# A two-layer encoder trunk on one core: the attention's products with v of all four blocks of rows in one group behind both softmaxes, with five buffers for transposed probabilities

## The chip, the cores and the metric

The kernel runs on one core of a Trainium2 chip. The core has a matrix engine (TensorE, PE in the profile; its loads of weights are PEld), a vector engine (DVE), a scalar engine (ACT), a general engine (GpSimd, POOL) and an engine that here only starts DMAs (SP). Each takes its own instructions in a fixed order and waits for the others by semaphores. The metric is the time of one execution on the device, in microseconds (us). The kernel before took 1608.74 us, the median of three runs (1607.14 to 1610.86).

## What is computed

Two groups of 512 tokens (group 0, group 1) go through the same two layers of width 1024: a bidirectional recurrent layer, then a gated neighbourhood attention with 16 heads of 64. The part that matters here, from the reference:

```python
qr = lax.dynamic_index_in_dim(qg, r, axis=1, keepdims=False)
kr = lax.dynamic_slice_in_dim(kb, rs, win_r, axis=1)
vr = lax.dynamic_slice_in_dim(vb, rs, win_r, axis=1)
...
s = jnp.einsum('bnqhd,bsnkhd->bhnqsk', qr, kr, preferred_element_type=f32)
s = jnp.where(mask, s + bias.astype(f32), NEG_INF)
p = jax.nn.softmax(s.reshape(s.shape[:4] + (-1,)), axis=-1).reshape(s.shape)
return jnp.einsum('bhnqsk,bsnkhd->bnqhd', p.astype(v.dtype), vr)
...
return (o.reshape(bsz, t, D_INNER) * jax.nn.silu(z)) @ w_o + b_o
```

The tokens stand in a grid of 8 rows and 64 columns, and every token attends to a window of 8 rows and 16 columns around it.

## The kernel before

**Layout.** The kernel keeps activations as 128 channels by 512 tokens, the tokens ordered by grid column. 128 channels are two heads, a *pair*; there are eight pairs in each group. A pair's 512 queries are four *blocks* of 128 tokens (16 grid columns), n = 0 to 3, and each block attends to 256 tokens that begin at column 0, 8, 24 or 32 (`cols`).

**One pair** is the generator `heads(s, p)`, s the group, p the pair:

- It loads the bias and q, k, v of the pair (DMAs from SP), transposes v (L1573) and copies it to `vtok` (L1574). `vtok` has seven slots of 128 tokens; the copy fills the even ones, and two DMAs from POOL (L1575, L1576) put together the odd ones, which hold tokens shifted by 64. Block n reads the slots `cols[n] // 8` and that plus 2: 0 and 2, 1 and 3, 3 and 5, 4 and 6.
- For each half, blocks (0, 1) and then (2, 3): four products q by k, two heads for each of two blocks, into a bank `sc` (L1588). Then for each block and head the softmax: bias and maximum (L1599), exponential and sum on ACT (L1602), reciprocal (L1603) and scaling (L1604) on DVE, and two transposes of 128 by 128 into a bank `pt` (L1606). ACT copies the transposed probabilities of a block, both heads, to a buffer `pts` (L1609).
- Then the eight products with v of the half (L1621) into the pair's one bank `po`, the block with the higher number first (`ns[::-1]`). Each product appears in the profile as two records, since its operands are 32-bit floats: a half is 16 records.
- Behind the second half, `po` is multiplied with the gate z (L1630), and the result is split into two halves of reduced precision (`os`) for the product with the attention's output matrix (`out1` for group 0, `last` for group 1).

The long products that all other matrix products consist of are three for each 128 channels of input (L457 to L459, in `last` L1708 to L1710): 128 by 128 weights by 512 columns. The products of a pair with 64 rows or 64 columns use a part of the array each, so the two heads run side by side: in the profile 64*128 for the scores and 128*64 for the products with v.

**Buffers.** The banks of this phase are `pg` 2, `pt` 2 (`PG, PT`), `po` 1, `sc` 1, `pm` 1. `pts` has three buffers (`NPT`), `vtok` two (`NK`), the softmax rows `sb` four (`NSB`). A buffer is written again when all who read it are done.

**What sets the order.** In this phase the order on each engine isn't written out by hand. A planner works it out when the kernel is built: it goes through simulated time and puts in line on each engine, among the instructions whose inputs and buffers are ready, the one with the best priority, which is the place in the source unless it is raised. `high_priority(HPA)`, 1000 places, raises the scores and the products with v; `behind(one, last)` keeps the order inside such a group. Transposes and copies have their place in the source.

**How it is interleaved.** In `rest`, generators of long products are advanced, and between their steps the attention's generator is advanced by some share: `run(g, (a, 0.9))` advances `a` 0.9 steps for each step of `g`. A step of `g` is three long products. For group 0, six pairs are queued at first; the input products of pairs 6 and 7 (32 steps each at 0.9, so 28 attention steps each) and group 1's first-layer output product (`out0(1)`, 64 steps at 1.0) carry 120 attention steps. A pair takes 15 steps. Behind `out0(1)`, what is left of the queue is emptied (`while queue: next(a)`), and then come `out1(0)` and group 1's norm. For group 1, the input products of one pair carry the attention of the pair before, 21 steps (32 at 0.66) for a pair in the middle, and the rest is emptied before `last`.

Of the kernel before, what the change touches and what calls it, by code (L numbers as in the profile page):

```python
# [20 lines left out]
P = 128  # L21
# [233 lines left out]
class Trunk:  # L255
# [8 lines left out]
    POST4 = 0.2  # L264
    TOK = True
    LAST = ("pg", "pg", "po", "pm")
    PG, PT, NK, NPT = 2, 2, 2, 3
    AHEAD, AHEADW, SCAN_A, SCAN_W = 0, 0, 300, 300
    NAB, NX, NR, NY, NSB, NBI = 2, 2, 2, 2, 4, 2
    NAK, NZ = 1, 1  # L270
# [1289 lines left out]
    def heads(self, s, p):  # L1560

        nc = self.nc
        vt, act, gps = nc.vector, nc.scalar, nc.gpsimd
        a = lambda tag, shape=(P, T), n=1, dt=F32: self.t(tag, shape, n, dt, self.ap)
        bias = a("bias", (P, 2, 3, 256), self.NBI)
        for h in range(2):
            self.load(bias[:, h].rearrange("p a b -> p (a b)"), self.a["rpb"][2 * p + h])
        q, k, v = (self.load(a(kind, n=2), self.sp[kind, s, p]) for kind in ("q1", "k1", "v1"))
        yield
        vtok = a("vtok", (P, 7, P), self.NK)  # L1570
        ps = self.p("pm", (P, 4, P))
        for j in range(4):
            nc.tensor.transpose(ps[:, j], v[:, j * P:(j + 1) * P], self.ident)  # L1573
        act.copy(vtok[:, 0:7:2], ps)  # L1574
        nc.gpsimd.dma_start(vtok[0:64, 1:6:2], vtok[64:128, 0:5:2])  # L1575
        nc.gpsimd.dma_start(vtok[64:128, 1:6:2], vtok[0:64, 2:7:2])  # L1576
        yield
        op = self.p("po", (P, 4, P))
        cols = (0, 8, 24, 32)
        for ns in ((0, 1), (2, 3)):  # L1580

            scs = self.p("sc", (P, 2, 2, 256))
            with self.tc.high_priority(self.HPA):
                last = None
                for n in ns:
                    for h in range(2):
                        hs = slice(64 * h, 64 * h + 64)
                        one = nc.tensor.matmul(  # L1588
                            scs[:, h, n % 2], q[hs, n * P:(n + 1) * P], k[hs, 8 * cols[n]:8 * cols[n] + 256], start=True, stop=True)
                        if last is not None:  # L1590
                            self.behind(one, last)
                        last = one
            pts = []
            for n in ns:
                pt = self.p("pt", (P, 2, 2, P))
                for h in range(2):
                    sb = a("sb", (P, 256), self.NSB)
                    mx = a("mx", (P, 4), 6)
                    vt.tensor_tensor_reduce(  # L1599
                        sb, scs[:, h, n % 2], bias[:, h, (0, 1, 1, 2)[n]], 1.0, -3.0e38, op0=ALU.add, op1=ALU.max, accum_out=mx[:, 0:1])  # L1600
                    vt.tensor_scalar(mx[:, 1:2], mx[:, 0:1], -1.0, None, op0=ALU.mult)  # L1601
                    act.activation(sb, sb, AF.Exp, bias=mx[:, 1:2], accum_out=mx[:, 2:3])  # L1602
                    vt.reciprocal(mx[:, 3:4], mx[:, 2:3])  # L1603
                    vt.tensor_scalar(sb, sb, mx[:, 3:4], None, op0=ALU.mult)  # L1604
                    for e in range(2):
                        nc.tensor.transpose(pt[:, h, e], sb[:, e * P:(e + 1) * P], self.ident)  # L1606
                    yield
                pts.append(a("pts", (P, 2, 2, P), self.NPT))
                act.copy(pts[-1], pt)  # L1609
                if n % 2 == 0:  # L1610
                    yield
            if ns[1] == 3:
                while ("z1", s, p) not in self.sp:
                    yield
                z = self.load(a("z1"), self.sp["z1", s, p])
            with self.tc.high_priority(self.HPA):
                last = None
                for n in ns[::-1]:
                    for e in range(2):
                        for h in range(2):  # L1620
                            one = nc.tensor.matmul(  # L1621
                                op[64 * h:64 * h + 64, n], vtok[:, cols[n] // 8 + 2 * e, 64 * h:64 * h + 64], pts[n % 2][:, h, e],
                                start=(e == 0), stop=(e == 1))
                            if last is not None:
                                self.behind(one, last)
                            last = one
            yield
        with self.tc.high_priority(self.HP[s] if p == NP - 1 else 0):
            o = self.tmp()
            vt.tensor_tensor(o, op.rearrange("p n t -> p (n t)"), z, op=ALU.mult)  # L1630
            lo, hi = (self.t("os", (P, T), 2 * NP, F32R, self.ap) for _ in range(2))
            o = self.halves(o, lo, hi)
        self.os[s].append(o)
        yield
# [447 lines left out]
```

## Time and profile before

| | us |
|---|---|
| median of three runs | 1608.74 |
| the profiled execution | 1607.96 |
| its span | 1606.2 |
| PE busy | 1512.5 |
| DVE busy | 1221.5 |
| ACT busy | 968.3 |
| attention of group 0, with long products, 1115 to 1274 | 159 |
| `out1(0)` and the norm of group 1, 1274 to 1339 | 65 |
| attention of group 1, with long products, 1339 to 1567 | 228 |

The span is the time between the first and the last instruction in the profile; the execution's time has some 2 us around it. Times in rows of the profile are from the span's start. A timeline's row has the start, the duration, the engine, the line of the kernel, the operation, output and inputs by the program's names, the form and the number of instructions merged into the row; a row of several instructions lasts from the first one's start to the last one's end. PE's instructions are pipelined, so the start of the next row tells more than a row's duration.

### The profile page before, as it was taken

What the parts mean: (1) busy time and instruction counts of PE and PEld (TensorE: products, weight loads), DVE (VectorE), ACT (ScalarE), POOL (GpSimd) and SP (SyncE); (2) the same over time, 40 slices, a digit from 0 to 9 for tenths busy, and PEclk for the clock granted to TensorE, in tenths of its full rate; (3) what the DMA queues carried; (4) which work ended last, traced back from release to release, by engine and by line L of the source; (5) the groups of instructions that cost most, each with busy time, mean ns of one, the idle gap of its engine ahead of it and who ended that gap; (6) DMA issues with size and microseconds to landing.
All of it is one profiled execution on the core that took longest, in us unless ns stands there. A gap on an engine that the chain in (4) does not pass through costs nothing.

```text
span 1606.2 us, 46435 instructions
## 1 busy us (share of the span) xinstructions
PE 1512.5 (94%) x18756; PEld 1170.9 (73%) x18756; DVE 1221.5 (76%) x2714; ACT 968.3 (60%) x1931; POOL 199.3 (12%) x368
## 2 busy tenths in 40 slices
PE   7998789998898999998999999999999999999998
PEld 6866667776666777766677777777777788777776
DVE  8996578689889798878799998655767585764664
ACT  6667455856757466676577665544667665554562
POOL 0000114301111012221000011000110002111110
PEclk9999899999999999999999999999999999999999
DMA  6359577777776787768777765465775347665553
GB/s 245 105 187 314 206 251 243 230 238 227 222 257 204 229 260 259 228 209 290 239 252 252 244 223 182 159 199 191 259 226 179 117 151 244 205 195 187 169 169 110
DMA packets 183670, 343.61 MB, mean 214 GB/s; under 512 B 25888, under 2 KB 58912, under 8 KB 183456
## 3 DMA queue, kind: packets, MB, share of 16 engines
q1 hardware_dynamic: 158272, 256.75, 50.1%
q0 software_dynamic: 25184, 83.90, 14.6%
q8 instruction: 147, 2.41, 0.6%
q14 instruction: 67, 0.55, 0.1%
HBM read 230.33 MB, written 107.09 MB: 210 GB/s over the span
## 4 chain that ended last, share of the span: by engine, by line
PE 68%; DVE 11%; DMA 9%; ACT 6%; issue 5%; SPq 0%; POOL 0%; DVEq 0%; ACTq 0%; POOLq 0%
PE pm L937 7%; PE pg L459 7%; PE pg L457 6%; PE pg L458 6%; PE pm L939 5%; PE pm L938 5%; PE pf L1249 3%; PE sc L1588 2%; PE po L1621 2%; PE pt L1606 2%; PE us L1368 2%; DMA cab<-dab 2%; DMA dab<-ab 2%; DVE ab L1071 2%; PE zy L457 2%
## 5 line engine op out<-in xcount | busy, mean ns | idle before, releaser
L937 PE MATMUL pm<-act,whi 128*128 128x512 f32 x672 | 296.0, 440 | 5.3 <-ACT vs L796 2.8
L939 PE MATMUL pm<-act,wlo 128*128 128x512 f32 x672 | 268.7, 400 | 12.8 <-DVE wlo L858 12.8
L938 PE MATMUL pm<-act,whi 128*128 128x512 f32 x672 | 268.3, 399 | 4.0 <-DVE act L884 3.9
L937 PEld LDWEIGHTS pm<-act,whi 128*128 128x128 f32 x672 | 128.6, 191 | 46.7 <-issue 10.8
L939 PEld LDWEIGHTS pm<-act,wlo 128*128 128x128 f32 x672 | 128.8, 192 | 43.7 <-DVE wlo L858 14.9
L457 PE MATMUL pg<-act,whi 128*128 128x512 f32 x384 | 156.5, 408 | 0.0
L459 PE MATMUL pg<-act,wlo 128*128 128x512 f32 x384 | 152.9, 398 | 0.0
L458 PE MATMUL pg<-act,whi 128*128 128x512 f32 x384 | 152.3, 397 | 0.0
L407 DVE TENSOR_TENSOR wlo<-raw,whi 128x512 fp32r<-128x512 f32 x150 | 102.7, 687 | 63.2 <-ACT whi L406 57.9
L938 PEld LDWEIGHTS pm<-act,whi 128*128 128x128 f32 x672 | 129.2, 192 | 28.4 <-DVE act L884 6.3
L406 ACT CAST whi<-raw 128x512 fp32r<-128x512 f32 x150 | 92.4, 617 | 94.5 <-PE pg L458 64.1
L858 DVE TENSOR_TENSOR wlo<-raw,whi 128x512 fp32r<-128x512 f32 x166 | 113.3, 684 | 29.5 <-ACT whi L856 28.3
L856 ACT CAST whi<-raw 128x512 fp32r<-128x512 f32 x166 | 102.2, 619 | 32.9 <-PE pm L938 25.2
L459 PEld LDWEIGHTS pg<-act,wlo 128*128 128x128 f32 x384 | 72.1, 188 | 18.2 <-issue 4.0
L1148 DVE TENSOR_TENSOR N<-etmp,N 128x30 f32<-128x30 f32 (+14 forms) x240 | 78.9, 329 | 4.6
L1146 DVE TENSOR_TENSOR etmp<-N 128x30 f32<-128x30 f32 (+14 forms) x240 | 78.7, 328 | 4.4
L458 PEld LDWEIGHTS pg<-act,whi 128*128 128x128 f32 x384 | 72.4, 189 | 13.1 <-issue 1.0
L457 PEld LDWEIGHTS pg<-act,whi 128*128 128x128 f32 x384 | 72.2, 188 | 12.5 <-issue 0.7
L1602 ACT ACTIVATE sb<-sb,mx 128x256 f32<-128x256 f32 x128 | 64.1, 503 | 19.8 <-DVE mx L1601 19.1
L1249 PE MATMUL pf<-cab 64*64 64x128 f32 (+1 forms) x2048 | 68.3, 269 | 0.8 <-issue 0.4
L1360 ACT COPY X<-us 64x256 f32<-64x256 f32 x128 | 46.8, 365 | 28.8 <-PE zy L1227 24.8
L1031 ACT ACTIVATE th<-pm,dv 128x512 f32<-128x512 f32 x64 | 43.9, 686 | 30.0 <-PE pm L1028 29.5
(402 smaller groups left out, 3501.7 us busy)
## 6 DMA issues: line engine op xcount, KB each, us to landing
dab<-ab POOLq DMA_DIRECT2D x32, 1024.0 KB, 7.4
cab<-dab SPq DMA_DIRECT2D x64, 512.0 KB
raw<-in_w_in_dram SPq DMA_DIRECT2D x128, 256.0 KB
bias<-in_rpb_dram SPq DMA_DIRECT2D x32, 384.0 KB
raw<-in_w_z_dram SPq DMA_DIRECT2D x32, 256.0 KB
raw<-in_w_k_dram SPq DMA_DIRECT2D x32, 256.0 KB
raw<-in_w_r_dram SPq DMA_DIRECT2D x32, 256.0 KB
k<-dk SPq DMA_DIRECT2D x32, 256.0 KB
```

Source lines behind the costliest of these rows:

```text
L406: self.nc.scalar.copy(hi, src)
L407: (eng or self.nc.vector).tensor_tensor(lo, src, hi.bitcast(F32), op=ALU.subtract)
L457: nc.tensor.matmul(ps, hi, x[k][0], start=(k == 0), stop=False)
L458: nc.tensor.matmul(ps, hi, x[k][1], start=False, stop=False)
L459: self.mm = nc.tensor.matmul(ps, lo, x[k][0], start=False, stop=(k == KT - 1))
L856: nc.scalar.copy(hi, raw[h])
L858: nc.vector.tensor_tensor(lo, raw.pop(h), hi.bitcast(F32), op=ALU.subtract)
L937: nc.tensor.matmul(ps, hi[:, at], xh, start=(k == 0), stop=False)
L938: nc.tensor.matmul(ps, hi[:, at], xl, start=False, stop=False)
L939: nc.tensor.matmul(ps, lo[:, at], xh, start=False, stop=(k == KT - 1))
L1148: vt.tensor_tensor(N[:, q + 1:, :q], tv, N[:, q + 1:, :q], op=ALU.add)
L1249: end = nc.tensor.matmul(st.f[half(a), h, 0, d, g] if st.last else st.f[half(a), h, :, d, g], ab[half(h), d, g, 2 * e[d] + 1 - a], rt if s ...
```

## The change

`pts` gets five buffers instead of three. The two groups of eight products with v are taken out of the loop over the halves; behind the loop stands one group of sixteen, which goes through the blocks in rising order, and reads `pts[n]` of the pair's four instead of `pts[n % 2]` of the half's two. The bank `po` is taken where that group begins and not at the pair's start. The wait for z and its load stand in front of the group as before. There is a `yield` behind each half, and one more behind the products, so a pair takes 16 steps.

```diff
-    PG, PT, NK, NPT = 2, 2, 2, 3
+    PG, PT, NK, NPT = 2, 2, 2, 5
...
-        op = self.p("po", (P, 4, P))
-        cols = (0, 8, 24, 32)
+        cols, pts = (0, 8, 24, 32), []
         for ns in ((0, 1), (2, 3)):
...
-            pts = []
             for n in ns:
                 pt = self.p("pt", (P, 2, 2, P))
...
-            if ns[1] == 3:
-                while ("z1", s, p) not in self.sp:
-                    yield
-                z = self.load(a("z1"), self.sp["z1", s, p])
-            with self.tc.high_priority(self.HPA):
-                last = None
-                for n in ns[::-1]:
-                    for e in range(2):
-                        for h in range(2):
-                            one = nc.tensor.matmul(
-                                op[64 * h:64 * h + 64, n], vtok[:, cols[n] // 8 + 2 * e, 64 * h:64 * h + 64], pts[n % 2][:, h, e],
-                                start=(e == 0), stop=(e == 1))
-                            if last is not None:
-                                self.behind(one, last)
-                            last = one
             yield
+        while ("z1", s, p) not in self.sp:
+            yield
+        z = self.load(a("z1"), self.sp["z1", s, p])
+        op = self.p("po", (P, 4, P))
+        with self.tc.high_priority(self.HPA):
+            last = None
+            for n in range(4):
+                for e in range(2):
+                    for h in range(2):
+                        one = nc.tensor.matmul(
+                            op[64 * h:64 * h + 64, n], vtok[:, cols[n] // 8 + 2 * e, 64 * h:64 * h + 64], pts[n][:, h, e],
+                            start=(e == 0), stop=(e == 1))
+                        if last is not None:
+                            self.behind(one, last)
+                        last = one
+        yield
         with self.tc.high_priority(self.HP[s] if p == NP - 1 else 0):
             o = self.tmp()
             vt.tensor_tensor(o, op.rearrange("p n t -> p (n t)"), z, op=ALU.mult)
```

## The prediction

> **What bounds the kernel now.** I read the page's busy shares first, then the busy times by stage, then the chain of work that ended last over the two attention stages, and last the timelines of TensorE (PE) and ScalarE (ACT) inside two pairs.
>
> ```profile
> span 1606.2 us, 46435 instructions
> PE 1512.5 (94%) x18756; PEld 1170.9 (73%) x18756; DVE 1221.5 (76%) x2714; ACT 968.3 (60%) x1931; POOL 199.3 (12%) x368
> 1115.00:1274.00 159.00, 159.00 (x995) 123.80 (x993) 107.92 (x399) 104.39 (x249) 16.10 (x27) 1.00 0.64 212
> 1339.00:1567.00 228.00, 228.00 (x1299) 178.69 (x1298) 142.45 (x457) 125.82 (x287) 32.08 (x56) 1.00 0.60 194
> 1567.00:1599.00 32.00, 31.92 (x137) 25.30 (x136) 15.60 (x29) 7.74 (x19) 0.00 (x0) 1.00 0.33 113
> ```
>
> The last three rows are stages: their length, then the busy time of PE, its weight loads, VectorE, ACT and GpSimd, the granted clock, the DMA share. The first two hold the attention of the two groups. PE is busy in all 159 and all 228 us, at full clock, and stays so until 1599, some 7 us before the end; VectorE and ACT have a third of the time free. The chain agrees:
>
> ```profile
> by line: PE pg L459 19.7%; PE pg L458 19.6%; PE pg L457 19.6%; PE sc L1588 12.4%; PE po L1621 10.3%; PE pt L1606 10.3%; PE pm L1573 2.2%; PE pm L939 2.0%; PE pm L937 1.9%; PE pm L938 1.9%; PE pm L485 0.4%
> ```
>
> That is the first group's stage: every entry is PE. So here time is what PE's instructions take back to back. An engine's wait that PE doesn't share is worth nothing, and whatever makes PE's own sequence longer is paid in full.
>
> **What a bunch of products with v costs PE.** The long products (L457 to L459) and the transposes (L1606) use the array as 128*128, the products with v (L1621) as 128*64, the scores (L1588) as 64*128.
>
> ```profile
> 1475.60 0.40 PE L458 MATMUL pg<-act,whi 128*128 128x512 f32 x1
> 1475.93 1.09 PE L1621 MATMUL po<-pts,vtok 128*64 128x128 f32 x16
> 1476.95 0.50 PE L459 MATMUL pg<-act,wlo 128*128 128x512 f32 x1
> 1477.29 0.39 PE L457 MATMUL pg<-act,whi 128*128 128x512 f32 x1
> 1477.52 0.40 PE L458 MATMUL pg<-act,whi 128*128 128x512 f32 x1
> ...
> 1229.67 0.70 PE L1588 MATMUL sc<-k,q 64*128 64x256 f32 x2
> 1230.30 1.10 PE L1621 MATMUL po<-pts,vtok 128*64 128x128 f32 x16
> 1231.32 1.13 PE L1588 MATMUL sc<-k,q 64*128 64x256 f32 x6
> 1232.38 0.87 PE L1606 MATMUL pt<-cc,sb 128*128 128x128 f32 x6
> ```
>
> Undisturbed, long products start 0.23 us apart (1477.29 to 1477.52). Around the bunch, 1475.60 to 1477.29 is 1.69 us for two of them, so the bunch takes 1.69 - 0.46 = 1.23 us: 1.02 between its own start and the next product's, and 0.21 around it. What of the 1.02 is work? The scores tell: two records (one product of 256 columns in two passes) took 0.63 us, six took 1.06. Six are two rounds, since the two heads run side by side; so a round costs 0.43 and a bunch 0.20 on top. A product with v has half the columns, so a round of 0.215, and sixteen records are four rounds: 0.86 of work, 0.16 of fixed cost. A bunch that stands alone thus costs **0.16 + 0.21 = 0.37 us** beyond its work; one that adjoins scores, only the 0.16.
>
> A rule of the Trainium skill stands behind this row: "TensorEngine Tiling (Array Packing)", section Key Properties, says that a change of the tiling mode, unlike a change of tile, drains the array. Two changes at the skill's constant of about 166 ns for one warm product ("TensorE: Matmul & The Clock Gate", section Single matmul latency) would make an estimate of 0.33 us, and 22 bunches 7.3 us where my rows will say 8.1.
>
> **The change part by part.** The arithmetic is the same: 16 products with v for each pair, as many scores, transposes, copies, DMAs. What moves is (1) the place of the products of the first two blocks, (2) their order, (3) the number of buffers, (4) one step of the generator.
>
> (1) and (2) decide. In the source there is one bunch of 16 products where there were two of 8. But the planner sets PE's order, and what it does with a product at raised priority can be read. Of a pair in the first group:
>
> ```profile
> 1240.58 0.59 ACT L1609 COPY pts<-pt 128x512 f32<-128x512 f32 x1 [0.29 <-PE pt L1606]
> 1244.02 0.58 ACT L1609 COPY pts<-pt 128x512 f32<-128x512 f32 x1
> 1250.75 1.07 ACT L1609 COPY pts<-pt 128x512 f32<-128x512 f32 x2 [1.47 <-PE pt L1606]
> ...
> 1247.35 1.13 PE L1588 MATMUL sc<-k,q 64*128 64x256 f32 x6
> 1248.41 1.09 PE L1621 MATMUL po<-pts,vtok 128*64 128x128 f32 x16
> 1249.43 0.70 PE L1588 MATMUL sc<-k,q 64*128 64x256 f32 x2
> 1255.70 1.09 PE L1621 MATMUL po<-pts,vtok 128*64 128x128 f32 x16
> ```
>
> and of a pair in the second:
>
> ```profile
> 1467.87 0.59 ACT L1609 COPY pts<-pt 128x512 f32<-128x512 f32 x1
> 1471.28 0.57 ACT L1609 COPY pts<-pt 128x512 f32<-128x512 f32 x1
> 1476.00 0.56 ACT L1609 COPY pts<-pt 128x512 f32<-128x512 f32 x1
> 1479.43 0.58 ACT L1609 COPY pts<-pt 128x512 f32<-128x512 f32 x1
> ...
> 1484.48 1.09 PE L1621 MATMUL po<-pts,vtok 128*64 128x128 f32 x16
> ```
>
> The products follow the copy of the probabilities they read by a steady distance: 1244.02 to 1248.41 is 4.4 us, the second copy of the double row (about 1251.3) to 1255.70 also 4.4, 1471.28 to 1475.93 (quoted above) 4.7, 1479.43 to 1484.48 5.1. And three scores of four stand ahead of the bunch at 1248.41 and one behind it: the planner cuts into a group as soon as something is ready. So raised products go where their operand gets ready, not where the source has them. Each half today stands as one bunch of 16 records because its order is backwards: the block whose copy is last goes first. The change counts upwards, block 0 first, and block 0 is ready while three softmaxes are still to come. Nothing else holds it: the output bank is freed by the multiplication with z of the pair before, which follows that pair's last products within 0.2 us of their end (1272.35 and 1273.50, quoted below).
>
> I therefore expect the products of each block about 4.7 us behind their own copy. In the second group's pair that is four bunches of 8 records: 1472.6, 1476.0, 1480.7, 1484.2. In the first group's pair, three: block 0 alone, block 1, and blocks 2 and 3 together, as their copies are back to back and block 3 is ready by the time block 2 has been put in line. Copies that are back to back show as a row with x2:
>
> ```profile
> 1143.08 1.08 ACT L1609 COPY pts<-pt 128x512 f32<-128x512 f32 x2 [2.82 <-PE pt L1606]
> ...
> 1561.03 1.05 ACT L1609 COPY pts<-pt 128x512 f32<-128x512 f32 x2
> ```
>
> These are the first and the last of nine such rows among the 64 copies. One more couple would join: blocks 0 and 1 of the very last pair, whose output bank is held until the pair before is multiplied with z:
>
> ```profile
> 1557.50 0.68 DVE L1630 TENSOR_TENSOR tmp<-po,z 128x512 f32<-128x512 f32 x1
> 1560.11 1.09 PE L1621 MATMUL po<-pts,vtok 128*64 128x128 f32 x16
> ```
>
> That makes 64 - 9 - 1 = **54 bunches where there are 32**, 22 more. At 0.37 us each: **+8.1 us**. The bounds of one more bunch are 0.16 us (it happens to adjoin scores, +3.5 in all) and the scores' own 0.20 + 0.21 = 0.41 (+9.0); I take 0.37, since block 0 and most of the others would stand among long products, like the bunch at 1475.93.
>
> Scores beside the products: today a split into 2 and 6 records costs 0.63 us, as each part pays a round and a drain. Block 1's products meet the scores at the same point as now, so these splits stay; I put nothing. Block 2's products, put in first, could open a new split in front of block 3; at worst 0.63 us in some eight pairs, 5 us; below nothing, one split less here or there, -2.
>
> (3) Five buffers instead of three: the copies don't wait for a buffer today but in the last pair, where the double row at 1561.03 stands behind the products at 1560.11. PE is full there, so a copy that is earlier hides behind long products: nothing. Without that cover it would be worth the copy's 0.58 us.
>
> (4) Each pair now takes 16 steps instead of 15, against 28 + 28 + 64 = 120 steps that the long products of the first group's stage give out: eight pairs needed exactly these 120. Eight steps of the last pair now come behind all of the second group's product with w_o. A step there is three long products, 0.69 us, so its end may slip by up to 5.5 us. Behind it wait the first products of the attention's output matrix:
>
> ```profile
> 1272.35 1.09 PE L1621 MATMUL po<-pts,vtok 128*64 128x128 f32 x16
> 1273.50 0.69 DVE L1630 TENSOR_TENSOR tmp<-po,z 128x512 f32<-128x512 f32 x1 [1.70 <-PE po L1621]
> 1274.87 0.69 DVE L407 TENSOR_TENSOR os<-tmp,os 128x512 fp32r<-128x512 f32 x1 [0.69 <-ACT os L406]
> 1279.20 0.62 PE L457 MATMUL pg<-os,whi 128*128 128x512 f32 x2
> ```
>
> The last pair's slice is complete at 1274.87 + 0.69 = 1275.6, and it is first needed at 1279.20, when both columns that have a bank have used up everything else: 3.6 us of cover. I take nothing, since what gets ready is put in line at once, wherever the source has it; the bounds are 0 and 5.5 - 3.6 = 1.9 us.
>
> **The sum:** +8.1. Of the profiled execution, whose time was 1607.96 us around its span of 1606.2, that makes 1616.1; the median of the three runs, 1608.74, is 0.8 above it, so of the median 1616.8.
>
> **The rivals.**
>
> *One bunch, as the source has it (faster).* If a product can't be put in line before the whole bunch's position is reached, 16 bunches vanish. Seven of today's first bunches adjoin scores (0.16 each), nine don't (0.37): 1.1 + 3.3. With the bunch go the splits of scores into 2 and 6 records around it, four at 0.63 us, of which this is the first and the one at 1247.35 the last; together -7 us, 1601.7.
> ```profile
> 1175.39 0.70 PE L1588 MATMUL sc<-k,q 64*128 64x256 f32 x2
> ```
>
> It decides from the point at which block 0's products are still behind block 3's copy. Against it: the scores of the next half, which the source has behind these products, get ahead of them at 1247.35.
>
> *Block 0 waits for v.* Odd slots of the transposed v come by two DMAs; block 1 needs them, block 0 doesn't. If it is made to wait all the same, blocks 0 and 1 go together in seven pairs of the second group: 15 more bunches, +5.5, 1614.2.
>
> *More splits or a stall between the groups.* The upper ends above: +8.1 + 5 + 1.9, at most 1623.8.
>
> *Hidden in PE.* A busy PE is modelled, and weight loads fill only 178.69 of 228 us (78%); if PE had slack between its products, the extra bunches would fall into it and the time stay at 1608.7. Against it: the starts 0.23 us apart on both sides of the bunch, widened by the whole of it. The Trainium skill, "Perfetto Trace Analysis", section Identifying the Most-Contended Engine, says to judge TensorE's headroom by weight loads, not by matmul time; by that rule a fifth of the stage is free and this rival would win.
>
> **How the numbers follow.** Forecast 0.62, with a range of its own of 1611.5 to 1621; block 0 waiting 0.12; more splits or a stall 0.08; hidden, or so few new bunches that it comes to the same, 0.09; one bunch 0.09. The range leaves out the one bunch and the far end of the splits, and reaches down into the hidden case: 1607 to 1622. A change under 0.2%, 3.2 us, can't be told from none in this kernel. Slower by more: 0.62 + 0.12 + 0.08, less a little for cheap bunches, 0.79; the same 0.12; faster 0.09.
>
> **What would show it.** L1621 in bunches of 8 records and single ones of 16, 54 or so in number and none of 64 records or of 32; block 0's about 4.7 us behind its copy; PE still busy throughout both stages, each longer, the first by some 3 us and the second by 5; an unchanged 7 us behind the last product. The prediction is wrong if the products of a pair stand in one row of 32 records, if the long products beside a short bunch show no gap, or if PE shows idle time around 1280.

## The result and the profile after

The changed kernel took 1625.35 us, the median of four runs (1624.13 to 1626.73); the kernel before, run beside it, took 1607.94, also the median of four runs (1606.85 to 1610.86). The ratio is 1.0112, 95% interval 1.0091 to 1.0133: **17.4 us slower**. The forecast was 8.1 us slower, so the direction came true and the size is over twice as large; it is also more than the 15 us that the prediction's worst rival allowed (8.1 + 5 + 1.9). Behind the change's edits the products with v are on L1620, the transposes on L1604, their copies on L1607, the scores on L1587.

The page of the changed kernel, its span and busy times:

```profile
span 1622.4 us, 46445 instructions
PE 1522.2 (94%) x18756; PEld 1164.7 (72%) x18756; DVE 1223.0 (75%) x2714; ACT 972.8 (60%) x1931; POOL 199.9 (12%) x368
```

The number of PE records is the same as before, and DVE, ACT and POOL are busy for less than 5 us more: no work was added. To see where the time lies, take **the stretch** from the first long product of the attention phase (the first L457 that writes into `pg`) to the start of the last one. It holds all of the attention and all long products beside it. The busy times by window over this stretch (start and end, length, then PE, its weight loads, DVE, ACT, POOL, granted clock, DMA share, GB/s), first of the kernel before:

```profile
1123.77:1598.52 474.75, 474.75 (x2704) 374.88 (x2703) 306.74 (x958) 274.36 (x619) 51.48 (x89) 1.00 0.57 186
```

and of the kernel after:

```profile
1121.51:1614.71 493.20, 490.69 (x2704) 373.33 (x2703) 307.91 (x958) 277.47 (x619) 51.67 (x89) 1.00 0.55 179
```

The stretch grew by 18.45 us. The spans of these two profiles differ by 16.2, since the stretch also began 2.3 us earlier. Nearly all of it is PE: 15.9 us more busy and 2.5 us idle, where there was no idle time at all. The granted clock in the stretch is 1.00 in both. What follows the last product is 7.7 us in both (1606.2 - 1598.52 and 1622.4 - 1614.71).

PE's timeline shows the mechanism that the prediction named. A pair of the second group, first the copies of the probabilities on ACT:

```profile
1478.98 0.59 ACT L1607 COPY pts<-pt 128x512 f32<-128x512 f32 x1 [0.29 <-PE pt L1604]
1482.22 0.59 ACT L1607 COPY pts<-pt 128x512 f32<-128x512 f32 x1 [1.02 <-PE pt L1604]
1487.70 0.59 ACT L1607 COPY pts<-pt 128x512 f32<-128x512 f32 x1 [0.61 <-PE pt L1604]
1491.02 0.58 ACT L1607 COPY pts<-pt 128x512 f32<-128x512 f32 x1
```

then PE's products with v of the same pair, with the long products on both sides of the first:

```profile
1483.17 0.39 PE L459 MATMUL pg<-act,wlo 128*128 128x512 f32 x1
1483.49 0.66 PE L1620 MATMUL po<-pts,vtok 128*64 128x128 f32 x8
1484.08 0.50 PE L457 MATMUL pg<-act,whi 128*128 128x512 f32 x1
1484.42 0.40 PE L458 MATMUL pg<-act,whi 128*128 128x512 f32 x1
...
1486.36 0.66 PE L1620 MATMUL po<-pts,vtok 128*64 128x128 f32 x8
...
1492.20 0.66 PE L1620 MATMUL po<-pts,vtok 128*64 128x128 f32 x8
...
1495.51 0.66 PE L1620 MATMUL po<-pts,vtok 128*64 128x128 f32 x8
```

Four bunches of 8 records, 4.5, 4.1, 4.5 and 4.5 us behind their own copies. The first has a long product 0.32 us ahead of it and the second long product after it starts 0.34 us behind the first: 1483.17 to 1484.42 is 1.25 us, of which two long products take 0.46 and two rounds of products 0.43, so 0.36 us is the price of this bunch.

In a pair of the first group the scores are among them:

```profile
1215.20 0.66 PE L1620 MATMUL po<-pts,vtok 128*64 128x128 f32 x8
1216.84 0.70 PE L1587 MATMUL sc<-k,q 64*128 64x256 f32 x2
1217.46 0.66 PE L1620 MATMUL po<-pts,vtok 128*64 128x128 f32 x8
1218.05 1.13 PE L1587 MATMUL sc<-k,q 64*128 64x256 f32 x6
1221.14 0.66 PE L1620 MATMUL po<-pts,vtok 128*64 128x128 f32 x8
1226.03 0.66 PE L1620 MATMUL po<-pts,vtok 128*64 128x128 f32 x8
...
1228.25 0.38 PE L1604 MATMUL pt<-cc,sb 128*128 128x128 f32 x2
1228.38 0.48 PE L457 MATMUL pg<-act,whi 128*128 128x512 f32 x1
...
1229.17 0.38 PE L1604 MATMUL pt<-cc,sb 128*128 128x128 f32 x2
```

Block 1's products again cut a group of scores (2 and 6 records). And the transposes come two records at a time among long products, where the kernel before had eight in a row:

```profile
1250.06 1.09 PE L1606 MATMUL pt<-cc,sb 128*128 128x128 f32 x8
```

The waits of PE over the stretch, as its timeline shows them in brackets, are these four:

```profile
1288.54 0.51 PE L457 MATMUL pg<-os,whi 128*128 128x512 f32 x1 [0.85 <-ACT oa L1643]
...
1572.83 1.10 PE L1620 MATMUL po<-pts,vtok 128*64 128x128 f32 x16 [1.02 <-DVE tmp L1629]
...
1574.65 0.98 PE L1604 MATMUL pt<-cc,sb 128*128 128x128 f32 x6 [0.37 <-DVE sb L1602]
...
1576.38 0.50 PE L1709 MATMUL pg<-act,os 128*128 128x512 f32 x1 [0.27 <-DVE os L407]
```

**A ledger of the stretch.** Every PE row of the stretch is charged with the time from its start to the next row's start, and each long product's time beyond 0.2285 us, about what it takes undisturbed, goes to the neighbour beside which it stands. In us:

| | before | after | difference |
|---|---|---|---|
| products with v, in 32 bunches, then 61 | 32.79 | 37.18 | +4.4 |
| long products ahead of and behind them, without idle time | 2.70 | 7.49 | +4.8 |
| scores, in 38 groups, then 42 | 37.42 | 40.24 | +2.8 |
| long products around scores | 3.06 | 4.03 | +1.0 |
| all transposes, in 111 groups, then 137, and the long products around them | 40.94 | 42.82 | +1.9 |
| idle | 0 | 2.5 | +2.5 |
| all else (the remainder) | | | +1 |

So there are 29 more bunches, at (4.4 + 4.8) / 29 = 0.32 us each: 9.2 us. The other half is in three places that the prediction put at nothing or didn't cost: the scores, the transposes and the idle time.

### The profile page after: what moved, and what is told of

The parts are those of the page before. It is cut to its first block, busy times and chain, and to the rows that moved or that the text cites. A ratio compares the mean times of both kernels' runs of the same rounds, so it can differ in the third digit from the quotient of the medians.

```text
span 1622.4 us, 46445 instructions
## 1 busy us (share of the span) xinstructions
PE 1522.2 (94%) x18756; PEld 1164.7 (72%) x18756; DVE 1223.0 (75%) x2714; ACT 972.8 (60%) x1931; POOL 199.9 (12%) x368
## 3 DMA queue, kind: packets, MB, share of 16 engines
q0 software_dynamic: 25184, 83.90, 14.5%
## 4 chain that ended last, share of the span: by engine, by line
PE 55%; DVE 8%; DMA 6%; issue 3%; ACT 3%; SPq 0%; POOL 0%; DVEq 0%; ACTq 0%; POOLq 0%
PE pg L457 6%; PE pg L459 6%; PE pg L458 6%; PE pm L937 5%; PE pm L938 4%; PE pm L939 4%; PE sc L1587 2%; PE pf L1249 2%; PE po L1620 2%; PE us L1368 2%; PE pt L1604 2%; PE zy L1321 1%; DMA cab<-dab 1%; PE zy L1372 1%; PE us L1348 1%
## 5 line engine op out<-in xcount | busy, mean ns | idle before, releaser
L457 PE MATMUL pg<-act,whi 128*128 128x512 f32 x384 | 162.1, 422 | 0.0
L458 PE MATMUL pg<-act,whi 128*128 128x512 f32 x384 | 152.8, 398 | 0.0
L407 DVE TENSOR_TENSOR wlo<-raw,whi 128x512 fp32r<-128x512 f32 x150 | 102.7, 687 | 57.8 <-ACT whi L406 43.7
L459 PEld LDWEIGHTS pg<-act,wlo 128*128 128x128 f32 x384 | 72.2, 188 | 17.4 <-issue 2.7
L457 PEld LDWEIGHTS pg<-act,whi 128*128 128x128 f32 x384 | 72.3, 188 | 16.0 <-issue 5.9
L1600 ACT ACTIVATE sb<-sb,mx 128x256 f32<-128x256 f32 x128 | 64.3, 503 | 30.6 <-DVE mx L1599 30.2
L1597 DVE CUSTOM_DVE_ANT_0 sb<-sc,bias 128x256 f32<-128x256 f32 x128 | 50.8, 421 | 29.1 <-PE sc L1587 17.5
```

What stands on the lines that cost most here:

```text
L407: (eng or self.nc.vector).tensor_tensor(lo, src, hi.bitcast(F32), op=ALU.subtract)
L457: nc.tensor.matmul(ps, hi, x[k][0], start=(k == 0), stop=False)
L458: nc.tensor.matmul(ps, hi, x[k][1], start=False, stop=False)
L459: self.mm = nc.tensor.matmul(ps, lo, x[k][0], start=False, stop=(k == KT - 1))
```

## The experiments

Whole times are set against runs of the kernel before that were taken beside them, so its median differs a little from one comparison to the next; the ratios and their intervals come from all the runs and need not be the quotient of the medians. The stretch is always set against the one profile of the kernel before. Whole times vary by several us from run to run, but the stretch hardly does (the last section shows it), so each kernel is judged by both.

**Only the order turned.** The kernel before, its two halves and its three buffers kept, the lower block first:

```diff
-                for n in ns[::-1]:
+                for n in ns:
```

> The kernel before with one edit: inside each half the products with v go through the blocks upwards (0, 1 and 2, 3) instead of backwards. Nothing is moved, three buffers, 15 steps. Theory A (the time is what PE pays for every bunch of products, 0.37 us where it stands alone, and 0.63 us for every split of scores): the order on PE now has 61 bunches instead of 32, by these prices about +13 us, so 1621 (1618 to 1623). Rival B (the cost comes from the place behind both softmaxes, the later bank or the five buffers): no change, 1608. Rival C (the cost comes from the 16th step, which lets the last pair of the first group end late): no change, 1608.

It took 1622.72 us against 1608.26: ratio 1.0096 (1.0064 to 1.0128), +14.5 us.

```profile
1120.42:1608.77 488.35, 487.64 (x2705) 371.46 (x2703) 307.36 (x958) 275.20 (x619) 51.58 (x89) 1.00 0.57 181
```

Of the 18.45 us of the stretch this one word makes 13.6, with 61 bunches as after the change. The lines of a pair of the first group read like the changed kernel's:

```profile
1228.16 0.66 PE L1621 MATMUL po<-pts,vtok 128*64 128x128 f32 x8
1229.81 0.70 PE L1588 MATMUL sc<-k,q 64*128 64x256 f32 x2
1230.43 0.66 PE L1621 MATMUL po<-pts,vtok 128*64 128x128 f32 x8
1231.02 1.13 PE L1588 MATMUL sc<-k,q 64*128 64x256 f32 x6
```

**The place kept, the order turned back.** The changed kernel, each half's later block first:

```diff
-            for n in range(4):
+            for n in (1, 0, 3, 2):
```

> The changed kernel with one edit: the blocks in the order 1, 0, 3, 2, which is the order of before, but all behind both softmaxes, with five buffers and 16 steps. Theory A: each couple's later block goes first, so 32 bunches as in the kernel before and about its time, 1608, plus at most 2.5 us of idle PE at the ends of the groups: 1606 to 1611. Rival B: the place is as in the changed kernel, so 1625. Rival C: 1611 or more, all of it idle time of PE around the first group's end.

1610.91 us against 1608.26: ratio 1.0015 (0.999 to 1.0039). The stretch is 475.77 us, 1.0 longer than before, with 32 bunches again. In this order the place behind both softmaxes, the later bank, five buffers and the 16th step together are worth about 1 us, of which 0.8 is idle. What makes the changed kernel slow needs the rising order.

**The last block first.** The changed kernel, wholly backwards:

```diff
-            for n in range(4):
+            for n in (3, 2, 1, 0):
```

> The changed kernel with one edit: the blocks go downwards, 3 to 0, so the block whose copy is last goes first. Theory A: nothing can be put in line before the last copy, so 16 bunches of 32 records; by the prices -5 us against the kernel before, and up to 2.5 us of idle PE at the ends: 1602 to 1606. Rival B: place, bank and buffers are as in the changed kernel, so 1625. Rival C: some 1611, with the first group's last pair late.

1609.01 us against 1608.26: ratio 1.0007 (0.9981 to 1.0033). That misses the gain expected of it. The bunches did join, 16 of 32 records, and PE is busy for 5.1 us less in the stretch; but 3.2 us of it are idle, so the stretch is only 1.9 us shorter, which the scatter of the whole times hides. In the profiled execution the stretch also began 8 us later than before, ahead of the attention:

```profile
1131.87:1604.71 472.84, 469.67 (x2705) 374.74 (x2703) 307.57 (x958) 275.50 (x619) 51.51 (x89) 1.00 0.58 187
```

Most of the idle time stands at the ends of the two groups, where the norm waits for DVE, and then `out1` of group 0 and `last` of group 1 wait for a bank to come free:

```profile
1285.24 0.91 PE L499 MATMUL pm<-tmp,ones 128*128 128x128 f32 x6 [1.08 <-DVE tmp L495]
1288.62 0.50 PE L457 MATMUL pg<-os,whi 128*128 128x512 f32 x1 [0.84 <-ACT oa L1643]
...
1574.79 0.50 PE L1707 MATMUL po<-h,os 128*128 128x512 f32 x1 [0.79 <-DVE tmp L1629]
```

That points to the 16th step, which the next three take apart.

**Rising order with 15 steps.** The changed kernel, without the step behind the second half:

```diff
-            yield
+            if ns[0] == 0:
+                yield
```

> The changed kernel with one edit: no step behind the second half, so that a pair takes 15 steps as before; blocks upwards, one group behind both softmaxes, five buffers. Theory A: the order on PE has 61 bunches and as many splits of scores as the run with only the halves turned upwards; PE's busy time in the stretch from the first product of the input projection to the end is 488 us as there, and the time 1621 (1618 to 1623): of the change's 18 us some 3 busy and 2 idle belong to the 16th step. Rival B (the place behind both softmaxes, the later bank, the buffers cost by themselves): as the changed kernel, 1625.

1619.52 us against 1605.71: ratio 1.0081 (1.0052 to 1.0111). The stretch is 487.80 us, 5.4 shorter than after the change and 0.5 shorter than with only the order turned, and both have 61 bunches and 40 groups of scores:

```profile
1131.26:1619.06 487.80, 487.41 (x2704) 371.57 (x2703) 307.53 (x958) 275.47 (x619) 51.58 (x89) 1.00 0.55 181
```

So the 16th step costs 5.4 us here: 2.1 of idle time, 2.5 in scores (40.24 - 37.75 in the ledger, two groups more), the rest around them. Place, bank and buffers cost nothing.

**Only the 16th step.** The kernel before, with one more step ahead of the multiplication with z:

```diff
+        yield
         with self.tc.high_priority(self.HP[s] if p == NP - 1 else 0):
```

> The kernel before with one edit: one more step behind the products with v, so 16 for a pair. Theory A: 32 bunches and one split of scores less, so PE is busy for the same 475 us; the last pair of the first group ends later and PE idles 0 to 2.5 us around it: 1607 to 1611. If the 16th step by itself is the larger part of the change's cost: 1616 or more.

1607.81 us against 1605.71: ratio 1.001 (0.9984 to 1.0035). The stretch is 476.74 us, +2.0, of which 1.8 is idle:

```profile
1286.82 0.50 PE L457 MATMUL pg<-os,whi 128*128 128x512 f32 x1 [0.84 <-ACT oa L1645]
...
1566.50 0.63 PE L1606 MATMUL pt<-cc,sb 128*128 128x128 f32 x4 [0.93 <-DVE sb L1604]
```

By itself the step makes the idle time and no new splits. Here it stands behind the products with v, in the changed kernel ahead of them; the run in the order 1, 0, 3, 2, with the step where the changed kernel has it, has no new splits either (37 groups of scores, 38 before). So the splits need the rising order too.

**Only the buffers.** The kernel before with five buffers:

```diff
-    PG, PT, NK, NPT = 2, 2, 2, 3
+    PG, PT, NK, NPT = 2, 2, 2, 5
```

> The kernel before with five buffers for transposed probabilities in place of three, nothing else. Theory A: PE's order is the same instruction for instruction, so 1608, with 474.7 us of PE in the stretch from the first product of the input projection. Rival B (buffers): a difference beyond 3 us to either side.

1607.43 us against 1605.71: ratio 1.0001 (0.9976 to 1.0026). The stretch is 474.69 us against 474.75. In the kernel before, two more buffers do nothing.

**The last block first, with 15 steps.** Both edits, the falling order and 15 steps, on the changed kernel:

```diff
-            yield
+            if ns[0] == 0:
+                yield
...
-            for n in range(4):
+            for n in (3, 2, 1, 0):
```

> The changed kernel with two edits: blocks downwards, 3 to 0, and no step behind the second half, so that a pair takes 15 steps as before. Theory A: 16 bunches of 32 records, fewer splits of scores than in the run with 16 steps (2 instead of 6 or so); by the prices -7.7 us against the kernel before: 1599 to 1602. Rival B: 1625. Rival C: as before, 1608, since with 15 steps nothing is late and a bunch costs nothing.

1600.50 us against 1608.26: ratio 0.9951 (0.9928 to 0.9974), **7.8 us faster than before**. The same kernel, measured a second time:

> The kernel with blocks downwards and 15 steps once more, in more rounds, since its first measurement spread over 17 us. Theory A: PE's stretch from the first product of the input projection to the last product 468.9 us as there, 6 us less than in the kernel before, and the time 4 to 9 us less. If the first result was chance: within 3 us.

gave 1599.68 against 1606.34, ratio 0.9956 (0.9931 to 0.9981). The stretches of the two:

```profile
1124.84:1593.71 468.87, 467.70 (x2704) 374.94 (x2703) 304.85 (x958) 275.15 (x619) 51.55 (x89) 1.00 0.59 188
```

```profile
1124.75:1593.33 468.58, 467.47 (x2705) 375.00 (x2703) 304.80 (x958) 274.97 (x619) 51.54 (x89) 1.00 0.57 189
```

They are 5.9 and 6.2 us shorter than before. A bunch now holds all four blocks, with unsplit scores and eight transposes in a row beside it:

```profile
1237.63 1.97 PE L1621 MATMUL po<-pts,vtok 128*64 128x128 f32 x32
1239.53 1.13 PE L1587 MATMUL sc<-k,q 64*128 64x256 f32 x8
1240.60 1.09 PE L1604 MATMUL pt<-cc,sb 128*128 128x128 f32 x8
```

This version beats both kernels. What the change's source seems to say, one bunch behind both softmaxes, is worth a gain when the block that gets ready last goes first and the pair keeps its 15 steps. Even so 1.1 to 1.2 us of its stretch are idle, most of it a wait for a bank in `out1`, as with 16 steps.

**As many bunches as possible.** The changed kernel with the products with v no longer raised, so that they take their place in the source among the long products:

```diff
-        with self.tc.high_priority(self.HPA):
+        with self.tc.high_priority(0):
```

> The changed kernel with one edit: the products with v get no raised priority, so the planner puts the long products between them: 173 bunches, most of a single product (two records), 141 more than before; the scores aren't split at all (32 groups). Theory A: at 0.37 us a bunch, less 4 us for splits that are gone: +49 us against the kernel before, 1657 (1645 to 1668). Rival (what costs is the splits of scores and idle PE, not the bunches): 1604 to 1612.

1672.99 us, the median of two runs, against 1605.71: ratio 1.0403 (1.0335 to 1.0472). The stretch is 538.36 us, +63.6, with 173 bunches, 143 of them one product of two records:

```profile
1470.35 0.43 PE L1620 MATMUL po<-pts,vtok 128*64 128x128 f32 x2
1470.71 0.49 PE L457 MATMUL pg<-act,whi 128*128 128x512 f32 x1
1471.14 0.43 PE L1620 MATMUL po<-pts,vtok 128*64 128x128 f32 x2
```

The price of a bunch holds far from 32 and 61, but the expected 49 us fell short. A product that stands alone has no product of the other head beside it, so it takes a whole round of 0.215 us where a pair of them shares one: 143 times 0.107 is 15.3 us, and 49 + 15.3 = 64.3, against 63.6 measured. From bunch to bunch is 0.79 us with one long product of 0.23 between: 0.56 us for one product with v. This reason was formed behind the run, but the rows bear it out. From the bunch's start to the next long product is 0.36 us here, 0.59 for a bunch of 8 records (1483.49 to 1484.08, after the change) and 1.02 for one of 16 (1475.93 to 1476.95, before). Taken as one, two and four rounds of 0.215, each leaves 0.15 to 0.16 of fixed cost; with half a round, the lone product would be 0.11 us shorter.

**The rising order held together.** The changed kernel, with the first product of a pair put behind the pair's last transpose, so that block 0 can't run ahead:

```diff
-                        nc.tensor.transpose(pt[:, h, e], sb[:, e * P:(e + 1) * P], self.ident)
+                        tr = nc.tensor.transpose(pt[:, h, e], sb[:, e * P:(e + 1) * P], self.ident)
...
-            last = None
+            last = tr
```

> The changed kernel with one edit: the first product with v is put behind the pair's last transpose (an order on PE, no wait), so blocks 0 to 2, though still first in rising order, can't be put in line before it. Theory A (a product goes where it gets ready, and bunches are what costs): 35 bunches instead of 61, twelve of them of blocks 0 to 2 together, one split of scores; PE busy about 1.3 us longer than in the kernel before, up to 2.5 us idle, so +1 to +4 us and far below the changed kernel's +18. Rival (the rising order or the place costs by itself): as the changed kernel, +17.

1611.97 us against 1606.34: ratio 1.0036 (1.0009 to 1.0064). The stretch is 480.50 us: with 35 bunches and 33 groups of scores the rising order costs 5.75 us against 18.45, so what made the change slow was the number of bunches and what comes with it, and not the order as such. But it is over the 1 to 4 us expected. Of the 5.75, 2.3 are idle, at the ends of the groups again:

```profile
1278.27 0.50 PE L457 MATMUL pg<-os,whi 128*128 128x512 f32 x1 [0.84 <-ACT oa L1643]
...
1558.87 0.50 PE L1707 MATMUL pg<-h,os 128*128 128x512 f32 x1 [1.42 <-DVE tmp L1543]
```

PE is busy 3.4 us longer. The long products right behind a bunch take 2.3 us more, since 27 of the 35 bunches have a long product right behind them, where it was 6 of 32. Fewer splits save 2.7 us in the scores, and the rest, transposes and other long products, takes some 3.8 more; why these do was not taken apart.

## Why the prediction was right in direction and wrong in size

**The step that failed** is the sum. It had one term, the bunches, and that term was nearly right: 8.1 us forecast, 9.2 measured. It put three others at nothing, and these make the other half: the scores (3.8 us), the transposes (1.9) and PE's idle time (2.5), with 1 us that stays unexplained. By the runs, the rising order alone makes 13.6 of the stretch's 18.45 us, the 16th step on top of it 5.4, and place, bank and buffers -0.5.

**What bounds the kernel** held. PE was full, and 15.9 of the 18.45 us by which the stretch grew are busy PE.

**That raised products go where their operand gets ready** held, with its numbers: 4.1 to 4.6 us behind their own copies in the rows shown, for the 4.7 forecast, in bunches of 8 records and none of 32 or 64. The rival "one bunch" fell for this kernel; its estimate, 7 us faster, is near what the falling order with 15 steps then brought (7.8 and 6.7 in the whole time, 5.9 and 6.2 in the stretch). The rival "block 0 waits for v" fell: its first bunch stands alone, as at 1483.49.

**The count of bunches** was 61 and not 54. What failed in it is that blocks 2 and 3 of the first group's pairs would go together "as their copies are back to back". In the kernel before, the transposes ahead of eight of the nine couples of copies stand in a row of five to eight; the one at 1250.06 stands right behind a bunch and a split of scores (1248.41, 1249.43). With the order turned, the transposes come in twos (1228.25, 1229.17), the copies come apart as well, and with them the products. The copies of the pair shown above, blocks 2 and 3:

```profile
1216.94 0.59 ACT L1607 COPY pts<-pt 128x512 f32<-128x512 f32 x1 [0.59 <-PE pt L1604]
1221.39 0.56 ACT L1607 COPY pts<-pt 128x512 f32<-128x512 f32 x1
```

They are 4.4 us apart, and their products followed at 1221.14 and 1226.03. The changed order took away the rows that the count was made from: with the order alone turned, the 111 groups of transposes are already 138. Only three bunches of 16 records are left.

**The price of a bunch** was a little high: 0.32 us on average (0.15 in it, 0.17 around it) against 0.16 + 0.21. The 0.37 holds for a bunch between two long products (0.36 above); 29 of the 61 bunches stand so, 6 of 32 before. Others stand beside transposes, and what the ledger books to those is not in the 0.32. The two errors nearly cancel: 29 times 0.32 is 9.2 us, 22 times 0.37 was 8.1. Beside it stands the Trainium skill's "TensorEngine Tiling (Array Packing)", section Key Properties, on the drain at a change of mode: the estimate of 0.33 us that the prediction made with it lies beside the 0.32 on average and the 0.36 of the bunch at 1483.49. That the change of mode is what costs this is argued; no run here shows it apart.

**"These splits stay; I put nothing"** failed. Six groups of scores were split before and ten are after, for 2.8 us, inside the bounds of -2 to 5; and scores that used to adjoin a bunch stand apart more often, 1.0 us, which was not in the sum. Of the 2.8 us, 2.5 come only where the 16th step meets the rising order, as the kernel with 15 steps shows.

**The transposes** were counted as unchanged: their number is, but they stand in 26 more groups, and the long product behind each such group pays: 1.9 us. The prediction priced the change of order for the instructions that it moves and not for those that stood in a row because of them.

**"(4) … I take nothing"** failed, in time and in mechanism. On top of the rising order the 16th step costs 5.4 us where 1.9 was the most allowed: 2.5 in scores, 2.1 idle and the rest around them. The cover that was read at 1279.20 shrank but held: the last slice is complete at 1283.47 + 0.69 = 1284.16 (DVE's L407) and first needed at 1285.82. What PE waits for in `out1`, 0.85 us at 1288.54, is a bank: both `pg` banks hold finished columns until ACT has copied one (L1643). Before, the eight products of the norm (L499) stood in that gap:

```profile
1280.57 1.05 PE L499 MATMUL pm<-tmp,ones 128*128 128x128 f32 x8
1281.38 0.48 PE L457 MATMUL pg<-os,whi 128*128 128x512 f32 x1
```

After the change they stand ahead of the last slice's products, and nothing is left for the gap:

```profile
1285.24 0.83 PE L499 MATMUL pm<-tmp,ones 128*128 128x128 f32 x6
1285.82 0.71 PE L457 MATMUL pg<-os,whi 128*128 128x512 f32 x2
1286.37 0.38 PE L499 MATMUL pm<-tmp,ones 128*128 128x128 f32 x2
```

The wait at this place (0.84 to 0.86 us, 0.61 without raised priority) is in every profile where the norm's products begin ahead of the last slice's, and in none of the others. The falling order with 15 steps is among the first, so it is not the 16th step's alone; why the planner puts the norm ahead was not looked into. That 0.85 lies inside the forecast's bounds of 0 to 1.9 is luck, since they were worked out for another wait. The end of the second group, which the prediction left out, has a stall of its own: at 1572.83 the last pair's products wait 1.02 us for the one output bank, until the pair before has been multiplied with z, and that multiplication had waited for the load of z:

```profile
1571.99 0.69 DVE L1629 TENSOR_TENSOR tmp<-po,z 128x512 f32<-128x512 f32 x1 [1.79 <-DMA z<-dz]
```

The transposes and the first split of `os` are late behind them (1574.65, 1576.38). The steps themselves were counted rightly; what depends on them at the other end was not looked up.

**"Hidden in PE"** fell. Weight loads fill 79% of the stretch before (374.88 of 474.75) and 76% after (373.33 of 493.20): the fifth that they leave took in none of the new bunches. The rule of the Trainium skill, "Perfetto Trace Analysis", section Identifying the Most-Contended Engine, to read headroom from the weight loads, does not agree with this trace, where 15.9 of the 18.45 us are busy PE and the other 2.5 are waits that the trace names. That section of the Trainium skill names a second measure beside the weight loads, the arithmetic done as a share of the peak; it was not worked out here.

**By stage:** up to the last product of `out1`, behind which the same work is done in both profiles, the stretch takes 190.4 us before and 199.9 after, so the first group's part cost 9.5 us more (0.85 of it idle), and the rest 9.0 (1.7 idle), against 3 and 5.

The whole is thus 8.1 + 1.1 (count and price of the bunches) + 3.8 (scores) + 1.9 (transposes) + 2.5 (idle) + 1 (the remainder), 18.4 us. The splits of scores, 2.8 us, stayed inside the bounds that the prediction gave them; the transposes and the stall at the end had none. The rival "more splits or a stall" named the right places, was given 0.08, and its most, 15 us, was still too little. One cause, instructions that get ready apart, moved most of these terms the same way, and so they belonged in the forecast, added up, and not in a rival with a small chance.

## What to carry to other kernels

Where a planner puts raised instructions in line as soon as they are ready, the order inside the group decides how they stand together: the one whose operand gets ready last goes first, and a group in order of readiness is strewn over the engine. On a full PE, count the bunches of another tile mode, not the products, and count again every neighbour (scores, transposes) whose own rows were held together by them. Where a generator's number of steps is changed, look at both ends of the phase that it feeds, and measure the stretch in the trace that the edit touches beside the whole time, which here hid 2 us of effect in over 10 us of scatter.

## What the runs showed of the hardware that was not expected

A product with v that stands alone costs 0.56 us of PE, five times the 0.107 us, half a round, that it adds beside the other head's product: 0.215 for a whole round, and 0.35 of fixed cost, about as much as a bunch of any length pays.

The scatter of the whole times (the falling order with 15 steps ran from 1592.87 to 1605.45 us in one comparison) lies ahead of the attention phase, as far as the profiles show. The stretch began between 1117.6 and 1131.9 us in the profiles here, though the instructions ahead of it are the same in kind and number (16052 records on PE); from there on, one order of instructions takes one time: 474.75 and 474.69 us for the kernel before and for it with five buffers, 468.87 and 468.58 for the falling order with 15 steps. The granted clock, 1.00 in the stretch of every profile, is lower ahead of it and goes along with the scatter: 0.98 on average in the profile whose stretch began first, 0.97 in the one whose stretch began last. Of 28 runs of the kernel before, the 13 with the higher granted clock (0.982 or more over the whole run) have a median of 1606.5 us, the other 15 of 1610.6. Whether the clock is the cause, and the only one, is not shown.
